# First quarter's modulation weights ahead of the rows; last quarter and gate as two float32r parts; gate in the second group

## The chip, the core and the metric

The kernel runs on one core of one Trainium2 chip. The metric is device time in microseconds, the median of three runs of the whole program: 2112.56 us (2109.44 to 2116.53). A profile of one further execution, with its trace, shows where the time goes. The engines are TensorE (PE, whose weight loads are shown apart as PEld), VectorE (DVE), ScalarE (ACT), GpSimd (POOL) and SyncE (SP), which issues nearly all transfers.

## The reference, cut to what matters

One inference step of one layer over 2048 prompt rows and 8 x 16 sample rows, all float32, width 1024. Nine conditioning vectors `c` (one for the prompt, eight for the samples) give a scale, a shift and a gate for every channel:

```python
mod = silu(c) @ w_ada + b_ada                 # (9, 3072), w_ada is 1024 x 3072
shift, scale, gate = split(mod, 3)
h = rmsnorm(x, norm_g) * (1 + scale) + shift  # needs scale and shift
z = h @ w_in + b_in                           # u, v, gate_a, glu_a, glu_b, gate_b, merge_a, merge_b
v_n = layernorm(gelu(v))
y_a = (gelu(u) * spatial(v_n) * silu(gate_a)) @ w_o_a
y_b = (silu(layernorm(conv31(glu_a * sigmoid(glu_b)))) * silu(gate_b)) @ w_o_b
m = sigmoid(merge_a) * y_a + sigmoid(merge_b) * y_b
y = rmsnorm(x + gate * (m @ w_out), final_g)  # needs gate
```

So `scale` and `shift` are wanted before the first product of the whole kernel, and `gate` only by the last stage of each group of rows.

## The kernel before, in words

**Rows and groups.** Activations lie transposed, channels on the partitions, in eight blocks of 128 channels (k = 0 to 7). The rows go in three groups (`GROUPS`): 768 prompt rows, 768 prompt rows, and 128 sample with the last 512 prompt rows. For each group `prepare` makes h (L772 to L811), `first_products` makes v, the gated convolution and the seven wide products, `branch_a`, `branch_b` and `output` do the rest. These products are numbered in steps from 1 on: the first group's stage of u and ga has the steps 33 to 48, the second group's products with w_in have 81 to 152, and their last stage (ma, mb, gb) 129 to 152.

**Arithmetic.** A product is either one float32 matmul, or several float32r matmuls on values written as the sum of a high and a low part. Nearly all products run on such parts (hh, hl, lh); the parts are made by one ACT and one DVE instruction (`halved`, `split`).

**The modulation.** `ada(name, q, ...)` (L470 to L518) makes one quarter (256 channels, so two blocks k) of scale, shift or gate: three transfers of `w_ada` (3, 3 and 2 blocks of 128 x 256 float32), the product with the nine vectors, an ACT copy out of PSUM, a small transpose by a matmul with `fold`, and two DVE instructions into `mod_scale`, `mod_shift` or `mod_gate`. The product has two forms. With `whole` each block is one float32 matmul of `cin` (9 columns) with 256 columns of weights (L482). Without it ACT writes the high part of the loaded weights (L487), DVE the low part (L489), and each block is two float32r matmuls of `cr`, the high and low parts of the nine vectors side by side (18 columns), with these (L496). In the kernel before all twelve calls are `whole`, so that `cr` is made and not used.

**Order.** All work is recorded as operations with an engine, a cost, what is read and written, a due time and at times a step before which it may not start (`nb`). `Plan.run` (L140) walks the five engines with a model of time and takes at each moment, on each engine, the ready operation of the smallest due time. The order is then fixed: each engine executes its queue strictly in that order, SP included, whose transfers wait in line behind any transfer that has to wait for a buffer. Operations that are due late (the 31 taps of the convolution on DVE, L947 and L951) fill what the model leaves free. Tiles come from a pool of 47 slots (`u`), and 9 units hold weights in parts (`ws`).

**The table that the change touches.** `ADA` gives for each quarter a due time and the forms of scale and shift. `XD = -6` is the due time of the loads of the group's rows (`load_x`, L746), and a quarter's transfers are due when its products are:

```python
ADA = [(-3, True, True), (-1.5, True, True), (-0.5, True, True), (0.5, True, True)]
GATE_AT = 36          # gate's four quarters: due at the steps 36, 40, 44, 48
```

Of the kernel before, what the change touches and what calls it, by code (L numbers as in the profile page):

```python
# [15 lines left out]
P = 128  # L16
D = 1024
# [15 lines left out]

ADA = [(-3, True, True), (-1.5, True, True), (-0.5, True, True), (0.5, True, True)]

# [6 lines left out]
CONV_STEP = (10, 10, 7)  # L42
GATE_AT = 36
LN_DUE = -6
# [213 lines left out]
def encoder_kernel(ctx: ExitStack, tc: tile.TileContext, xT, hist0, cT, w_ada, w_cols, w_v,  # L258
# [14 lines left out]
    op = plan.op  # L273
# [55 lines left out]
    cin = kv([P, KC, 9], "cin")  # L329
    cr = K([P, KC, 18], "cr", F32R).v  # L330
# [8 lines left out]
    def dma(out_fn, in_ap, writes, nbytes, due=0.0, nb=-1, reads=(), extra=0.0):  # L339
        return op("sp", nbytes / 340e3 + extra, lambda: nc.sync.dma_start(out=out_fn(), in_=in_ap),  # L340
                  writes=writes, reads=reads, due=due, nb=nb, lat=3.5)
# [7 lines left out]
    def new_step():  # L349
# [7 lines left out]
       reads=[vec], writes=[vec], due=-9)  # L357
    op("pool", 0.5, lambda: make_identity(nc, ident.t), writes=[ident])
    op("dve", 0.1, lambda: nc.vector.tensor_tensor(fold.t, ident.t[:, :9], ident.t[:, 9:18], op=ALU.add),
       reads=[ident], writes=[fold], due=-9)  # L360
    op("pool", 0.3, lambda: nc.gpsimd.memset(ones.t, 1.0), writes=[ones])
    op("act", 0.3, lambda: nc.scalar.activation(ones_r.t, ones.t, AF.Copy), reads=[ones], writes=[ones_r],
       due=-6)
    op("pool", 0.2, lambda: nc.gpsimd.memset(half.t, -0.5), writes=[half])
    op("act", 0.3, lambda: nc.scalar.activation(cin.t, cin.t, AF.Silu), reads=[cin], writes=[cin],
       due=-9, func="silu")
# [101 lines left out]
    AW = 256  # L468

    def ada(name, q, at, due, whole):  # L470


        ps = bank(f"ada{name}{q}")
        for ks in (range(0, 3), range(3, 6), range(6, 8)):
            m = len(ks) * AW
            w = slot("wa")
            dma(lambda w=w, m=m: w.t[:, :m], w_ada[:, at + ks[0] * AW:at + ks[0] * AW + m], [w], m * P * 4, due=due,
                nb=due - 2 if name == "gate" else -1)
            if whole:
                def mm4(w=w, ks=ks):  # L480
                    for z, k in enumerate(ks):
                        nc.tensor.matmul(ps.t[:9, :AW], cin.t[:, k, :], w.t[:, z * AW:(z + 1) * AW],  # L482
                                         start=(k == 0), stop=(k == KC - 1))
                op("pe", len(ks) * 0.22, mm4, reads=[w, cin], writes=[ps], due=due)
                continue
# [7 lines left out]
            def mm(wh=wh, wl=wl, ks=ks):  # L493
                for z, k in enumerate(ks):
                    for i, x in enumerate((wh, wl)):
                        nc.tensor.matmul(ps.t[:18, :AW], cr.t[:, k, :], x.t[:, z * AW:(z + 1) * AW],  # L496
                                         start=(k == 0 and i == 0), stop=(k == KC - 1 and i == 1))
            op("pe", len(ks) * 0.22, mm, reads=[wh, wl, cr], writes=[ps], due=due)
        a = slot("ada")
# [807 lines left out]
    for q in range(4):  # L1307
        due, scale_whole, shift_whole = ADA[q]
        ada("scale", q, 4 * q * D, due, scale_whole)
        ada("shift", q, (4 * q + 2) * D, due, shift_whole)  # L1310
    h = prepare(0, due=0, nb=-1, dr=DR)
    mixing_setup()
    for q in range(4):
        ada("gate", q, (16 + 2 * q) * D, GATE_AT + 4 * q, True)

# [74 lines left out]
```

## Time and profile before

| | |
|---|---|
| median of 3 runs | 2112.56 us (2109.44 to 2116.53) |
| the profiled execution | 2110.4 us, of which its span, first to last instruction, 2108.7 us |
| mean granted TensorE clock | 0.992 of full speed |
| PE busy | 2060.6 us, 98% |
| DVE busy | 1693.0 us, 80% |
| ACT busy | 931.0 us, 44% |
| memory traffic | 255 GB/s over the span |

The program is bound by TensorE nearly throughout. TensorE's first instruction stands at 14.46 us, so this is most of its idle time. Matmuls are pipelined and the end of one is modelled, so what a matmul costs is read from the start of one to the start of the next, not from its own duration. In the trace each float32 matmul of `ada` has two records, so that "x6" is a chunk of three.

### The profile page before, as it was taken

How to read it: one execution, taken by the hardware profiler on the slowest of the kernel's cores; microseconds unless marked ns; L12 is line 12 of the kernel's file. 1: busy time of each engine (PE TensorE's matmuls, PEld its weight loads, DVE VectorE, ACT ScalarE, POOL GpSimd, SP SyncE). 2: the span in 40 equal slices, each digit the busy share in tenths (PEclk: the TensorE clock that was granted, in tenths of full speed). 3: DMA queues.
4: the chain of work that ended last, by engine and by line, in shares of the span. 5: the costliest groups of instructions: out<-in, count | busy, mean ns of one | idle time of the engine just before them, and what ended most of it. 6: DMA issues, size and time to landing. Idle time of an engine off the chain costs nothing.

```text
span 2108.7 us, 33303 instructions
## 1 busy us (share of the span) xinstructions
PE 2060.6 (98%) x12810; PEld 1966.2 (93%) x12810; DVE 1693.0 (80%) x2407; ACT 931.0 (44%) x1356; POOL 89.5 (4%) x107
## 2 busy tenths in 40 slices
PE   7999999999999999999999999999999999999997
PEld 3999998999979999999998889999999999888997
DVE  5759988999899969688547899769999974956855
ACT  3354455455642343444446432434544544523432
POOL 0000000000100000000001010000000011010000
PEclk9999999999999999999999999999999999999998
DMA  8538777688975477887889876599989999376463
GB/s 328 205 141 295 260 298 270 225 312 294 318 252 204 137 264 247 279 262 246 285 262 324 312 218 181 174 342 335 335 300 319 335 314 342 119 232 221 154 196 118
DMA packets 190927, 540.58 MB, mean 256 GB/s; under 512 B 22064, under 2 KB 39728, under 8 KB 190768
## 3 DMA queue, kind: packets, MB, share of 16 engines
q1 hardware_dynamic: 180256, 511.11, 68.3%
q0 software_dynamic: 10512, 27.33, 7.4%
q8 instruction: 101, 1.65, 0.3%
q14 instruction: 58, 0.48, 0.1%
HBM read 375.47 MB, written 162.89 MB: 255 GB/s over the span
## 4 chain that ended last, share of the span: by engine, by line
PE 87%; DMA 6%; DVE 3%; issue 2%; ACT 0%; SPq 0%; POOL 0%; POOLq 0%; DVEq 0%; ACTq 0%
PE v L1032 9%; PE ob L615 9%; PE out L615 7%; PE bga L660 5%; PE bgla L660 5%; PE bu L660 5%; PE oa L615 4%; PE bglb L660 4%; PE bma L660 4%; PE bmb L660 4%; PE acga L660 3%; PE acu L660 3%; PE acgla L660 3%; PE acma L660 3%; PE bgb L660 3%; PE acglb L660 3%
## 5 line engine op out<-in xcount | busy, mean ns | idle before, releaser
L951 DVE SCALAR_TENSOR_TENSOR dw<-gb,cw,dw 128x768 f32<-128x768 f32 (+1 forms) x720 | 658.5, 924 | 37.8 <-ACT dw L936 32.2
L384 DVE TENSOR_TENSOR w<-ra,w 128x1024 fp32r<-128x1024 f32 x112 | 121.6, 1087 | 37.3 <-ACT w L382 36.3
L382 ACT ACTIVATE wh<-wr 128x1024 fp32r<-128x1024 f32 x88 | 91.9, 1053 | 133.7 <-PE ob L615 76.5
L382 ACT ACTIVATE w<-ra 128x1024 fp32r<-128x1024 f32 x112 | 105.6, 947 | 61.6 <-PE acgla L660 17.4
L384 DVE TENSOR_TENSOR wl<-wr,wh 128x1024 fp32r<-128x1024 f32 x88 | 106.9, 1216 | 3.3 <-ACT wh L382 3.3
L384 DVE TENSOR_TENSOR w<-rb,w 128x512 fp32r<-128x512 f32 x112 | 75.4, 685 | 40.6 <-ACT w L382 40.4
L382 ACT ACTIVATE w<-rb 128x512 fp32r<-128x512 f32 x112 | 67.9, 626 | 77.5 <-PE acglb L660 13.0
L947 DVE SCALAR_TENSOR_TENSOR dw<-gsb,cw,dw 128x128 f32<-128x128 f32 x240 | 82.5, 344 | 0.9 <-ACT dw L940 0.9
L1047 ACT ACTIVATE v<-v 128x768 f32<-128x768 f32 (+1 forms) x24 | 19.4, 810 | 110.4 <-DVE v L1043 94.4
L691 ACT ACT_TABLE_LOAD x50 | 64.2, 1283 | 0.9
L1230 DVE TENSOR_TENSOR mbb<-ob,mbb 128x768 f32<-128x768 f32 (+1 forms) x24 | 21.8, 910 | 51.0 <-PE ob L615 51.0
L671 ACT ACTIVATE u<-bu,vec 128x384 f32<-128x384 f32 (+1 forms) x48 | 26.9, 561 | 58.7 <-PE bu L660 58.6
L671 ACT ACTIVATE glb<-bglb,vec 128x384 f32<-128x384 f32 (+1 forms) x48 | 27.0, 562 | 57.4 <-PE bglb L660 57.0
L671 ACT ACTIVATE gla<-bgla,vec 128x384 f32<-128x384 f32 (+1 forms) x48 | 27.0, 563 | 51.3 <-PE bgla L660 48.0
L671 ACT ACTIVATE ga<-bga,vec 128x384 f32<-128x384 f32 (+1 forms) x48 | 26.9, 560 | 47.4 <-PE bga L660 46.7
L671 ACT ACTIVATE ma<-bma,vec 128x384 f32<-128x384 f32 (+1 forms) x48 | 27.0, 562 | 44.5 <-PE bma L660 43.0
L671 ACT ACTIVATE gb<-bgb,vec 128x384 f32<-128x384 f32 (+1 forms) x48 | 26.9, 561 | 35.9 <-PE bgb L660 33.0
L671 ACT ACTIVATE mb<-bmb,vec 128x384 f32<-128x384 f32 (+1 forms) x48 | 26.8, 559 | 32.6 <-PE bmb L660 32.1
L1277 DVE SCALAR_TENSOR_TENSOR x<-out,mod_gate,x 128x768 f32<-128x768 f32 (+1 forms) x24 | 20.1, 836 | 26.0 <-PE out L615 18.6
L1180 DVE TENSOR_TENSOR mab<-oa,mab 128x768 f32<-128x768 f32 (+1 forms) x24 | 21.7, 906 | 20.6 <-DMA mab<-away_ma__232 5.6
L382 ACT ACTIVATE w<-rs 128x1024 fp32r<-128x1024 f32 x28 | 29.6, 1056 | 16.0 <-DVE rs L445 9.2
L384 DVE TENSOR_TENSOR w<-rs,w 128x1024 fp32r<-128x1024 f32 x28 | 34.1, 1220 | 3.1 <-ACT w L382 1.1
(1068 smaller groups left out, 7190.5 us busy)
## 6 DMA issues: line engine op xcount, KB each, us to landing
w<-kept SPq DMA_DIRECT2D x224, 512.0 KB, 5.4
kept<-w SPq DMA_DIRECT2D x112, 512.0 KB, 4.0
ra<-in_w_cols SPq DMA_DIRECT2D x84, 512.0 KB, 6.6
wr<-in_w_cols SPq DMA_DIRECT2D x80, 512.0 KB, 6.2
rb<-in_w_cols SPq DMA_DIRECT2D x28, 512.0 KB, 5.9
rb<-in_w_cols SPq DMA_DIRECT2D x56, 256.0 KB, 5.3
x<-in_xT SPq DMA_DIRECT2D x32, 384.0 KB, 7.4
wa<-in_w_ada SPq DMA_DIRECT2D x24, 384.0 KB, 7.0
```

Source lines behind the costliest of these rows:

```text
L382: op("act", c_act(n, 0.1), lambda: nc.scalar.activation(hi_ap(), src_ap(), AF.Copy), reads=[src], writes=[hi], due=due)
L384: op("dve", c_dve(n), lambda: nc.vector.tensor_tensor(lo_ap(), src_ap(), hi_ap().bitcast(F32), op=ALU.subtract), reads=[src, hi], writes=[ ...
L615: nc.tensor.matmul(ps.t[:, z, :cw_], a.t[:, ks], b.t[:, c0:c0 + cw_], start=first and i == 0, stop=last and i == 2)
L660: nc.tensor.matmul(acc(), a.t[:, o + k * P:o + (k + 1) * P], b.t[:, xo:xo + nh], start=first and k == 0 and i == 0, stop=k == 3 and i == 2 ...
L671: op("act", c_act(nh, 0.28), lambda: nc.scalar.activation(half(i, z), B(), f, bias=col(bias, i)), reads=[bk, vec], writes=[out[i].part(z)] ...
L691: op("act", c_act(nh), lambda: nc.scalar.activation(half(1, 1), half(1, 1), func), reads=[out[1].part(1)], writes=[out[1].part(1)], due=st ...
L947: op("dve", c_dve(ns), lambda q=q: nc.vector.scalar_tensor_tensor(dw.t[:, :ns].rearrange("p (s l) -> p s l", l=LS), g3()[:, :, q:q + LS], ...
L951: op("dve", c_dve(npr), lambda q=q: nc.vector.scalar_tensor_tensor(dw.t[:, ns:n], g.t[:, q:q + npr], cw.t[:, j, q:q + 1], dw.t[:, ns:n], o ...
L1032: nc.tensor.matmul(o(), a.t[:, sl], view(b)[:, k % 4, :], start=state["n"] == 0, stop=state["n"] == 3 * KC - 1, skip_group_check=True)
L1180: op("dve", c_dve(n), lambda m=m, b=(lambda ps=ps, m=m: banks(ps, m, n)): nc.vector.tensor_tensor(b()[1], b()[0], b()[1], op=ALU.mult), re ...
L1230: op("dve", c_dve(n), lambda m=m, b=(lambda ps=ps, m=m: banks(ps, m, n)): nc.vector.tensor_tensor(b()[1], b()[0], b()[1], op=ALU.mult), re ...
L1277: op("dve", c_dve(bn), lambda j=j, x=x, ps=ps, bn=bn: nc.vector.scalar_tensor_tensor(x.t[:, :bn], ps.t.rearrange("p a b -> p (a b)")[:, :b ...
```

## The change

Four edits, with no other line touched:

1. `ADA_LOAD` gives the transfers of a quarter a due time of their own. For the first quarter it is -8 and -7.9, ahead of the rows' -6; for the other three it is what it was.
2. The last quarter of scale and shift is no longer `whole`.
3. All four quarters of gate are no longer `whole`, and are due at the steps 131, 135, 139 and 143, in place of 36 to 48.
4. The model's cost of a block becomes 0.43 (whole) and 0.24 (parts), in place of 0.22 for both.

```diff
-ADA = [(-3, True, True), (-1.5, True, True), (-0.5, True, True), (0.5, True, True)]
+ADA = [(-3, True, True), (-1.5, True, True), (-0.5, True, True), (0.5, False, False)]
+
+ADA_LOAD = [(-8, -7.9), (-1.5, -1.5), (-0.5, -0.5), (0.5, 0.5)]
...
-GATE_AT = 36
+GATE_AT = 131
...
-    def ada(name, q, at, due, whole):
+    def ada(name, q, at, due, whole, load=None):
...
-            dma(lambda w=w, m=m: w.t[:, :m], w_ada[:, at + ks[0] * AW:at + ks[0] * AW + m], [w], m * P * 4, due=due,
-                nb=due - 2 if name == "gate" else -1)
+            dma(lambda w=w, m=m: w.t[:, :m], w_ada[:, at + ks[0] * AW:at + ks[0] * AW + m], [w], m * P * 4,
+                due=due if load is None else load, nb=due - 2 if name == "gate" else -1)
...
-                op("pe", len(ks) * 0.22, mm4, reads=[w, cin], writes=[ps], due=due)
+                op("pe", len(ks) * 0.43, mm4, reads=[w, cin], writes=[ps], due=due)
...
-            op("pe", len(ks) * 0.22, mm, reads=[wh, wl, cr], writes=[ps], due=due)
+            op("pe", len(ks) * 0.24, mm, reads=[wh, wl, cr], writes=[ps], due=due)
...
-        ada("scale", q, 4 * q * D, due, scale_whole)
-        ada("shift", q, (4 * q + 2) * D, due, shift_whole)
+        ada("scale", q, 4 * q * D, due, scale_whole, ADA_LOAD[q][0])
+        ada("shift", q, (4 * q + 2) * D, due, shift_whole, ADA_LOAD[q][1])
...
-        ada("gate", q, (16 + 2 * q) * D, GATE_AT + 4 * q, True)
+        ada("gate", q, (16 + 2 * q) * D, GATE_AT + 4 * q, False)
```

What the planner makes of it, at three places. Line numbers are two higher in the changed kernel.

SP's queue at the start of the program: before, the eight loads of rows `x` come first, and the first quarter's weights `wa` behind them.

```order
L340 DMA vec<-in_vecs 128x144
L746 DMA x_41_342<-in_xT 128x768
...
L746 DMA x_48_371<-in_xT 128x768
L340 DMA wa_376<-in_w_ada 128x768
L340 DMA wa_381<-in_w_ada 128x768
L340 DMA wa_386<-in_w_ada 128x512
```

And now, the same queue:

```order
L342 DMA vec<-in_vecs 128x144
L342 DMA wa_342<-in_w_ada 128x768
L342 DMA wa_348<-in_w_ada 128x768
L342 DMA wa_350<-in_w_ada 128x512
L342 DMA wa_352<-in_w_ada 128x768
L342 DMA wa_356<-in_w_ada 128x768
L342 DMA wa_363<-in_w_ada 128x512
L748 DMA x_53_366<-in_xT 128x768
```

The six transfers of the first quarter went past the eight of the rows; the order behind these is the same.

TensorE's queue around the first product of the kernel (`v_0_0`, of the first column block of v). Before: `adascale_21` is the third quarter's scale, `adashift_26` its shift, `adascale_31` and `adashift_36` the last quarter's; these stand between or behind the first products of v.

```order
L482 MATMUL adascale_21_526<-wa_508,cin 9x256 x2
L1032 MATMUL v_0_0_134_550<-wh_518,h0h_499 128x256
L1032 MATMUL v_0_0_134_550<-wh_518,h0l_514 128x256
...
L482 MATMUL adashift_26_561<-wa_516,cin 9x256 x3
...
L482 MATMUL adascale_31_608<-wa_554,cin 9x256 x3
...
L482 MATMUL adashift_36_646<-wa_615,cin 9x256 x2
```

Now, with `adascale_31` and `adashift_42` for the last quarter:

```order
L484 MATMUL adascale_21_524<-wa_488,cin 9x256 x2
L484 MATMUL adashift_26_532<-wa_511,cin 9x256 x2
L508 MATMUL adascale_21_524<-fold,ada_572 128x9 x2
L1034 MATMUL v_0_0_170_581<-wh_486,h0h_539 128x256
...
L498 MATMUL adascale_31_613<-wah_564,cr 18x256
L498 MATMUL adascale_31_613<-wal_585,cr 18x256
...
L498 MATMUL adashift_42_709<-wah_631,cr 18x256
L498 MATMUL adashift_42_709<-wal_716,cr 18x256
```

The third quarter's shift moved wholly ahead of the first product of v, and the last quarter is in short matmuls among the products of v.

SP's queue in the second group, as its stage of ma, mb and gb begins; before, kept parts of weights `w` and raw weights `ra` and `rb` follow each other here:

```order
L340 DMA rb_8987<-in_w_cols 128x512
L435 DMA w_9005<-kept_154 128x1024
L435 DMA w_9026<-kept_154 128x1024
L340 DMA ra_9030<-in_w_cols 128x1024
L435 DMA w_9080<-kept_157 128x1024
L340 DMA rb_9083<-in_w_cols 128x512
L435 DMA w_9099<-kept_157 128x1024
L435 DMA w_9131<-kept_157 128x1024
```

And now, from the same `rb` on:

```order
L342 DMA rb_8943<-in_w_cols 128x512
L437 DMA w_8961<-kept_154 128x1024
L437 DMA w_8982<-kept_154 128x1024
L342 DMA ra_8986<-in_w_cols 128x1024
L342 DMA wa_9036<-in_w_ada 128x768
L437 DMA w_9039<-kept_157 128x1024
L437 DMA w_9055<-kept_157 128x1024
L342 DMA wa_9072<-in_w_ada 128x768
L342 DMA wa_9078<-in_w_ada 128x512
```

The twelve transfers of gate, which stood in the first group's stage of u and ga, now stand here among the kept weights.

## Rows read from the trace of the kernel before

**Rows 1.** The page's table of engines: busy us, share of the span, instructions

```profile
PE 2060.6 (98%) x12810; PEld 1966.2 (93%) x12810; DVE 1693.0 (80%) x2407; ACT 931.0 (44%) x1356; POOL 89.5 (4%) x107
```

**Rows 2.** Chain that ended last in 0 to 110: start us, us, what

```profile
5.83 8.50 DMA wa<-in_w_ada
...
14.46 2.72 PE adascale L482 x6
17.18 1.79 PE xs L529 x12
...
28.54 0.37 PE psx L551
...
39.41 0.90 PE v L1032 x6
40.31 1.39 PE adashift L482 x6
...
43.64 0.55 PE v L1032 x3
44.19 0.96 PE adashift L482 x4
...
59.52 0.54 PE adashift L506 x4
60.06 9.83 PE v L1032 x81
```

**Rows 3.** A stretch of 5 us: busy by engine, TensorE's granted clock, DMA share, GB/s

```profile
30.00:35.00 5.00, 4.75 (x23) 2.17 (x22) 3.76 (x6) 1.98 (x4) 0.00 (x0) 1.00 1.04 414
```

**Rows 4.** Timeline of ACT: start us, us, engine line op, operands [idle before]

```profile
11.49 2.75 ACT L773 ACTIVATE xsq<-x 128x768 f32<-128x768 f32 x3 [0.15 <-DMA x<-in_xT]
30.62 0.49 ACT L554 ACTIVATE bcx<-psx 128x384 f32<-128x384 f32 x1 [0.17 <-PE psx L552]
```

**Rows 5.** Timeline of DVE at the start of the program

```profile
10.41 5.21 DVE L776 TENSOR_TENSOR xsum<-xsum,xsq 128x768 f32<-128x768 f32 x5 [1.22 <-ACT xsq L773]
...
23.17 0.48 DVE L513 TENSOR_SCALAR mod_scale<-adascale,vec 128x9 f32<-128x9 f32 x2 [2.29 <-PE adascale L506]
...
61.58 1.01 DVE L810 SCALAR_TENSOR_TENSOR h6l<-x,mod_shift,h6h 128x768 fp32r<-128x768 f32 x1
62.51 1.01 DVE L810 SCALAR_TENSOR_TENSOR h7l<-x,mod_shift,h7h 128x768 fp32r<-128x768 f32 x1
...
72.84 0.42 DVE L1039 TENSOR_TENSOR v<-v,bvA 128x256 f32<-128x256 f32 x1 [0.66 <-PE v L1032]
```

**Rows 6.** Timeline of PE: one chunk of gate among float32r products; the stall at 70 us

```profile
70.39 0.39 PE L1032 MATMUL v<-wh,h2h 128*128 128x256 f32 x1 [0.52 <-DVE v L1039]
...
277.29 0.34 PE L660 MATMUL acga<-h3h,w 128*128 128x384 f32 x1
277.55 1.46 PE L482 MATMUL adagate<-wa,cin 128*9 128x256 f32 x6
278.95 0.44 PE L660 MATMUL bga<-t3h,w 128*128 128x384 f32 x1
279.23 0.34 PE L660 MATMUL bga<-t3l,w 128*128 128x384 f32 x1
```

**Rows 7.** Longer stretches: group one's gates, its neighbours, group two's last stage

```profile
277.40:393.00 115.60, 115.60 (x625) 101.45 (x624) 99.53 (x131) 58.71 (x85) 1.05 (x1) 1.00 0.74 267
...
450.00:500.00 50.00, 50.00 (x287) 50.00 (x286) 47.95 (x60) 28.39 (x41) 0.84 (x1) 1.00 0.70 253
...
1000.00:1050.00 50.00, 50.00 (x288) 50.00 (x287) 27.19 (x30) 21.18 (x30) 0.86 (x1) 1.00 0.87 284
```

**Rows 8.** Transfers on the page: KB each, median us from issue to landing

```profile
wa<-in_w_ada SPq DMA_DIRECT2D x24, 384.0 KB, 7.0
```

**Rows 9.** Stretches of 10 us around the step from group one to two

```profile
580.00:590.00 10.00, 6.94 (x27) 5.36 (x26) 5.38 (x6) 4.75 (x7) 0.00 (x0) 0.73 1.05 329
590.00:600.00 10.00, 10.00 (x55) 8.73 (x55) 10.00 (x12) 6.83 (x8) 0.00 (x0) 0.93 1.03 413
```

## The prediction

> **What bounds the kernel now.** I read the page's table of engines first: PE is busy for 98% of the span and DVE for 80% [rows 1], so a change pays where it takes time from TensorE's queue, or from a wait in front of it. Next comes the chain that ended last in the first 110 us [rows 2]. Until 14.33 us it is a wait for the first `wa`, and from 14.46 us nearly all PE: float32 chunks of the modulation, first alone, then, from the first product of v at 39.34 us on, between products of v. Two matters are to be seen in it. A float32 chunk of three blocks takes 1.39 us and one of two 0.96, while a float32r matmul with the same 256 columns takes 0.12 us (81 in 9.83). And v is held up by queue order: modulation stands ahead of it and in it. Third, the stretch of the four gates, 277 to 393 us [rows 7]: PE is busy for all 115.6 us, so what leaves it there is time. The first of the chunks in it [rows 6] shows what one really costs.
>
> Times below are made against the profiled execution: 2110.4 us, of which 2108.7 are its span. The median shown, 2112.56 us, is 2.2 us more; I subtract the gain from the median.
>
> **Gate: removed from the first group.** A product of 384 columns takes 0.17 us from start to start (0.34 for two). The product before the chunk starts at 277.29, so the next one would start at 277.46; it starts at 278.95, and its successor 0.28 later, 0.11 more than usual [rows 6]. The chunk thus costs 278.95 - 277.46 + 0.11 = 1.60 us, which is 1.39 and 0.21 for the change of form. By the same 0.2, a chunk of two costs 1.16 and the pair of small transposing matmuls 0.75 (0.54 and 0.2). A quarter is 1.60 + 1.60 + 1.16 + 0.75 = 5.1 us, and four are 20.4 us of PE out of the first group.
>
> Added to the second group: per quarter 16 float32r matmuls of 256 columns, 16 x 0.12 = 1.92 us, with no change of form, and the same 0.75 for the transpose: 2.7 us, four times 10.7. Net on PE: **9.8 us saved**. The trace has no float32r matmul with 18 columns of weights. Its bounds are 0.12 us, the row of the same 256 columns with 128 columns of weights, and the float32 block's 1.39 / 3 = 0.46. I take 0.12: only the width of the weights differs.
>
> What hides the rest: in the second group each quarter adds three ACT and three DVE instructions (0.9, 0.9 and 0.6 us, by the 0.93 of a DVE instruction of 768 elements [rows 5] and the 0.92 of ACT's squares [rows 4]), some 10 us each over four quarters. DVE is busy for 27.2 of 50 us there and ACT for 21.2 [rows 7], PE for all 50. If that cover were gone, it would cost up to these 10 us. In the first group DVE, 99.5 of 115.6 us now, gets a stage some 20 us shorter, so about 96% busy. That is what 450 to 500 us shows already, 47.95 of 50 with PE at 50.00 [rows 7], so I take all 20.4 us. The order also sends six convolution taps out of that stage to later ones.
>
> **First quarter's weights ahead of the rows.** The six transfers are 2.1 MB, 5.2 us at the 0.4 MB per us that the start shows [rows 3]. The rows' loads come that much later: the last sum of squares, now done at 15.62 [rows 5], is done near 20.8. The second quarter's first weights are the fifteenth large transfer in place of the ninth, so 14.33 + 5.2 = 19.6 us. What PE gets for it is the first quarter's 7.5 us (twice 1.39 + 1.39 + 0.96) between 5 and 18 us, where it mostly stood still.
>
> From 19.6 us PE's queue runs without a pause, by the new order: second quarter 7.5; sums of the squares 1.8; four broadcasts 1.1 (0.37 + 0.18, twice); two transposes 1.1; third quarter, now scale and shift, 7.5; one transpose 0.5. That is 19.5 us, with the changes of form 19.9: the first product of v is at **39.5 us**, 0.2 later than before. Its operands are there: the broadcast ends near 31.5 (before at 31.1 [rows 4]), because the later rows meet a wait that is gone, 2.29 us in which DVE stood at `mod_scale` ahead of the broadcast's operands [rows 5].
>
> **Last quarter in parts.** What counts is how much modulation is left behind the first product. Before: nine chunks (six of 1.39, three of 0.96), four transposes of 0.54 and ten returns to v at 0.2 each (0.55 for three matmuls instead of 0.35) [rows 2]: 8.3 + 2.9 + 2.2 + 2.0 = 15.4 us. As a check, v's first column block ends at 72.7 [rows 5]: 33.4 us are 144 x 0.12 = 17.3 of v, 15.4, and a stall of 0.6 [rows 6]. After: three transposes with their returns, 2.2, and 32 parts at 0.12, 3.8: 6.0 us. The gain is 15.4 - 6.0 - 0.2 = **9.2 us**.
>
> Its cover is DVE. From 31.5 us on it has sixteen instructions for h and six low parts (14.9 + 5.0 at 0.93 and 0.62), two low parts of weights (2.4) and the modulation's small ones (1.5): done at 55.3, with its waits for the transposes by 57. PE first wants the last h behind 108 products of the lower six blocks and the 6.0 us, at 39.5 + 13.0 + 6.0 = 58.5. Before, the last h was done at 63.5. So 1.5 us are to spare; past that, each us that DVE is late costs one, at most the 5.0 of the new low parts. The DVE work that was done before 63 and is now behind it (some 3 us of sums for the combined operands) meets the later column blocks of v, where DVE waits for PE.
>
> **Two rules to weigh.** While all engines only load, the trace moves 414 GB/s [rows 3]. The Trainium skill (DMA: Bandwidth & Descriptors, Specifications) gives a core some 358 GB/s from memory; by this the 2.1 MB would take 5.9 us and the sum would lose 0.7. The trace disagrees, and I stay with the row. The other rule is about the clock, and a rival below.
>
> **Sum.** 9.8 + 9.2 = 19.0 us: span 2089.7, execution 2091.4, and on the median 2112.56 - 19.0 = **2093.6 us**.
>
> **Rivals.**
> - *TensorE's clock falls in the new gaps.* Now PE works early, then has a gap of some 2 us before 19.6. In the trace, in a stretch where PE stood for 3.1 of 10 us, the granted clock was 0.73 of full speed and in the next ten 0.93 [rows 9]: a mix of the 1.2 and 2.4 GHz levels that cost 2.7 + 0.7 = 3.4 us. The first chunk of the kernel took 2.72 in place of 1.39 [rows 2], though the granted clock reads full there. So 1.3 to 3.4 us are lost at 19.6: up to 2097.0. Against it: the gap is short. The Trainium skill (TensorE: Matmul & The Clock Gate, HAM oscillation — how this bites in real kernels) has a rule for it, that idle gaps of TensorE throttle its clock to half until it has been busy for a while; rows 9 agree.
> - *The rows come too late.* If the row statistics hold PE's queue at the sums or the broadcast, the 5.2 us of delay reach the first product: 2098.8. For it: all of h hangs on them. Against it: PE has modulation to do until 29 us.
> - *Gate's transfers collide.* Here SP's queue waits for PE to free weight units, memory moves 284 GB/s at 0.87 share [rows 7], and one `wa` takes 7.0 us to land [rows 8]. An ACT instruction that waits for it holds up the copies out of PSUM behind it, a transfer ahead of kept weights delays these. 4.2 MB at 0.39 are 10.8 us if none of it is hidden: 2104.4. Against it: the order places parts several products ahead of their use, and the same transfers in the first group cost PE nothing [rows 7].
> - *DVE becomes the bound.* If DVE's 16.1 idle us in the first group's stage [rows 7] are latencies that stay, little of the 20.4 comes out (1.6, the eight small instructions), while the second group still pays 10.7, and the start keeps 63.5 - 57 = 6.5: 2.6 us slower, 2115.2. It decides once DVE's work there exceeds the 95 us that PE has left. Against it: the neighbours at 96%.
> - *An 18-column part costs what a float32 block does* (slower). At 0.46, a quarter costs 16 x 0.34 = 5.4 us more than taken, six of them 32.6: 13.6 us slower, 2126.2. The point of no gain is 0.12 + 19.0 / 96 = 0.32 us a matmul. Against it: float32r with 128 columns of weights runs at 0.12.
>
> **How the numbers follow.** Forecast 0.64 (its own range 2089 to 2098), clock 0.08, rows 0.08, transfers 0.08, DVE 0.07, dear parts 0.03, rest 0.02. The range 2087 to 2105 takes in the first four and, downward, a first product a few us earlier together with a median as near to the profiled run as 2.2 us allow. A measurement of this kernel tells 0.3%, 6.3 us, from no change: faster is below 2106.2. That is the first four and little else, 0.87; DVE and what lies near it are the same, 0.09; slower 0.04.
>
> **What would show it.** In the profile after: PE's first chunk near 5 us; the first product of v at 39 to 40; DVE's last copy of v's first block near 63.5 in place of 72.8; no modulation on PE between 260 and 380; parts 0.12 apart in the second group, and PE still busy for 50 of 50 us there. Wrong would be a first product past 42, PE waits for `wal` or for h6 and h7, a clock under 1.00 between 15 and 40, or PE idle where gate's parts stand.

## The result

Four runs of the changed kernel took 2097.66 us in the median (2094.37 to 2099.14), four of the kernel before 2113.61: the ratio is 0.9924, with 0.9908 to 0.9941 as its 95% interval. That is 16.0 us, 12.5 to 19.4, less. 2093.6 was predicted. The profiled run took 2096.98 us, its span 2095.1 against 2108.7: 13.6 us, and the traces account for these.

Where they came from is read from the starts of the same instructions in both timelines of PE. All times are us from the start of the span. "v" is the first product of v, "bglb" the first of the seven wide products of a group, "bu" the first product of the first group's u, "oa" the first product of the first group's output of branch a, "sums" the column sums of the second group's rows (`xs`).

| first start of | v | bglb, group 1 | bu | oa | sums | bglb, group 2 | bglb, group 3 | end of span |
|---|---|---|---|---|---|---|---|---|
| before | 39.34 | 123.99 | 254.22 | 566.45 | 602.84 | 716.80 | 1343.74 | 2108.7 |
| after | 44.48 | 119.00 | 249.01 | 541.47 | 580.40 | 694.60 | 1331.67 | 2095.1 |
| lead | -5.1 | 5.0 | 5.2 | 25.0 | 22.4 | 22.2 | 12.1 | 13.6 |

So the start gave 5.0, the first group without its gates 20.0 (5.0 to 25.0); the step to the second group took 2.8, the gates in the second group 10.1; the last 1.5 come behind the third group's bglb, a stretch that takes from 762.1 to 766.2 us in the profiles of this study whatever the edit: this spread is no smaller, so they are not put down to the change.

**The profile after.** The page's table of engines, as in [rows 1], shows PE with 10.7 us less work and DVE with 14.1 more:

```profile
PE 2049.9 (98%) x12810; PEld 1970.5 (94%) x12810; DVE 1707.1 (81%) x2425; ACT 940.6 (45%) x1374; POOL 97.3 (5%) x107
```

The chain that ended last in the first 60 us answers to [rows 2] (start, us, what):

```profile
3.13 5.95 DMA wa<-in_w_ada
9.13 2.73 PE adashift L484 x6
...
18.13 0.65 issue
18.78 0.35 DVE mod_shift L520 x2
19.13 0.88 DVE xsum L778
...
22.23 0.97 DVE xsum L778
23.33 2.69 PE xs L531 x12
26.02 2.66 PE adascale L484 x6
28.68 2.10 PE adashift L484 x6
...
37.00 1.39 PE adascale L484 x6
...
44.55 0.90 PE v L1034 x6
...
54.10 0.69 PE adashift L498 x6
```

Two things are new in it. From 18 to 23 us the chain runs over DVE, which adds up the squares of the rows, and no longer over PE. And behind it PE is slow: the sums take 2.69 us (1.79 before), a chunk 2.66 (1.39 at 37.00). Stretches of the same trace (us, busy PE, PEld, DVE, ACT, POOL, TensorE's granted clock, DMA share, GB/s) show why, and answer to [rows 9]:

```profile
15.00:20.00 5.00, 3.62 (x20) 1.94 (x19) 2.99 (x7) 3.96 (x7) 0.00 (x0) 1.00 1.03 414
20.00:25.00 5.00, 3.25 (x12) 1.98 (x11) 2.87 (x3) 0.34 (x1) 0.00 (x0) 0.50 1.07 388
25.00:30.00 5.00, 5.00 (x15) 2.29 (x16) 2.24 (x5) 0.00 (x0) 1.34 (x1) 0.50 1.04 409
30.00:35.00 5.00, 4.73 (x23) 2.10 (x21) 1.96 (x4) 2.64 (x4) 0.00 (x0) 0.98 1.04 414
272.20:371.30 99.10, 99.10 (x568) 99.10 (x567) 95.18 (x120) 57.80 (x82) 1.05 (x1) 1.00 0.76 274
1000.00:1050.00 50.00, 50.00 (x293) 48.81 (x292) 31.99 (x39) 23.81 (x35) 0.00 (x0) 1.00 0.79 261
570.00:580.00 10.00, 3.27 (x20) 2.62 (x18) 10.00 (x12) 5.53 (x8) 0.00 (x0) 0.82 1.02 390
580.00:590.00 10.00, 9.60 (x43) 8.68 (x44) 9.88 (x14) 0.78 (x1) 2.06 (x1) 0.67 0.70 249
```

The granted clock is at its lower level, 1.2 of 2.4 GHz, from 20.0 to 30.2 us. Ahead of this PE had stood still for 1.3 us (until 19.39); the clock fell 0.6 us into the chunk that followed, so that the second stop, 1.75 us ahead of the sums, came when it was low already. It rose with PE at work without a stop since 23.33. The stretch 272.2 to 371.3 is the old place of the gates [rows 7]: PE is busy for all of it, DVE for 96%. From 1000 to 1050 the gates stand in it, and PE is busy for 50 of 50. From 570 on lies the step between the groups, with PE idle for 6.7 of 10 us.

The gate's parts on PE's timeline, in place of the chunk in [rows 6], start 0.12 us apart, and the product behind them starts 0.12 after the last; its own successor, at 963.90, keeps the usual 0.18:

```profile
962.85 0.34 PE L662 MATMUL bmb<-t23h,w 128*128 128x384 f32 x1
963.02 0.28 PE L498 MATMUL adagate<-wah,cr 128*18 128x256 f32 x1
963.13 0.28 PE L498 MATMUL adagate<-wal,cr 128*18 128x256 f32 x1
...
963.60 0.28 PE L498 MATMUL adagate<-wal,cr 128*18 128x256 f32 x1
963.72 0.34 PE L662 MATMUL acmb<-h0h,w 128*128 128x384 f32 x1
```

### The profile page after: what moved, and what is told of

Read it like the earlier page. It is cut to its first block, busy times and chain, and to the rows that moved or that the text cites. A ratio compares the mean times of both kernels' runs of the same rounds, so it can differ in the third digit from the quotient of the medians.

```text
span 2095.1 us, 33328 instructions
## 1 busy us (share of the span) xinstructions
PE 2049.9 (98%) x12810; PEld 1970.5 (94%) x12810; DVE 1707.1 (81%) x2425; ACT 940.6 (45%) x1374; POOL 97.3 (5%) x107
## 4 chain that ended last, share of the span: by engine, by line
PE 87%; DMA 7%; DVE 4%; issue 1%; ACT 0%; SPq 0%; DVEq 0%; POOLq 0%; ACTq 0%
PE v L1034 9%; PE ob L617 9%; PE out L617 7%; PE oa L617 5%; PE bu L662 5%; PE bga L662 5%; PE bglb L662 4%; PE bma L662 4%; PE bgla L662 4%; PE bgb L662 4%; PE bmb L662 4%; PE acu L662 3%; PE acga L662 3%; PE acglb L662 3%; PE acma L662 3%; PE acgla L662 3%
## 5 line engine op out<-in xcount | busy, mean ns | idle before, releaser
L953 DVE SCALAR_TENSOR_TENSOR dw<-gb,cw,dw 128x768 f32<-128x768 f32 (+1 forms) x720 | 657.0, 922 | 21.3 <-ACT dw L938 16.2
L1049 ACT ACTIVATE v<-v 128x768 f32<-128x768 f32 (+1 forms) x24 | 19.4, 810 | 103.1 <-DVE v L1045 89.6
L384 ACT ACTIVATE w<-rs 128x1024 fp32r<-128x1024 f32 x28 | 29.6, 1057 | 18.5 <-DVE rs L447 10.9
```

What stands on the lines that cost most here:

```text
L384: op("act", c_act(n, 0.1), lambda: nc.scalar.activation(hi_ap(), src_ap(), AF.Copy), reads=[src], writes=[hi], due=due)
L953: op("dve", c_dve(npr), lambda q=q: nc.vector.scalar_tensor_tensor(dw.t[:, ns:n], g.t[:, q:q + npr], cw.t[:, j, q:q + 1], dw.t[:, ns:n], o ...
```

## The experiments

Two questions were open: which edit gave what, and what took 4.2 us at the start and 2.8 between the groups. The table has the first starts of the same instructions, us, and the times; a ratio is to runs of the kernel before on the same chip.

| kernel | v | bglb 1 | oa | sums | bglb 2 | bglb 3 | span | median | ratio, interval |
|---|---|---|---|---|---|---|---|---|---|
| last_only | 38.84 | 118.02 | 560.33 | 597.16 | 710.10 | 1336.09 | 2101.2 | 2103.17 | 0.9958, 0.9945 to 0.9970 |
| gate_only | 41.09 | 125.72 | 548.90 | 587.55 | 702.89 | 1339.22 | 2102.5 | 2104.22 | 0.9966, 0.9954 to 0.9979 |
| rows_first | 33.88 | 117.66 | 540.01 | 579.59 | 694.13 | 1331.16 | 2093.3 | 2097.89 | 0.9937, 0.9923 to 0.9950 |
| gate_whole | 40.03 | 114.56 | 537.02 | 575.92 | 690.12 | 1336.94 | 2102.4 | 2106.97 | 0.9975, 0.9963 to 0.9986 |
| gate_early | 44.81 | 119.34 | 554.75 | 593.21 | 708.12 | 1336.31 | 2099.9 | 2100.11 | 0.9938, 0.9925 to 0.9952 |
| warm | 43.76 | 118.29 | 540.78 | 579.27 | 694.23 | 1332.10 | 2097.6 | 2097.93 | 0.9936, 0.9923 to 0.9949 |
| warm_all | 43.04 | 117.57 | 540.13 | 579.63 | 694.86 | 1332.19 | 2095.8 | 2097.81 | 0.9925, 0.9912 to 0.9938 |
| after_again | 44.03 | 118.56 | 541.03 | 580.03 | 694.15 | 1330.74 | 2095.6 | 2099.00 | 0.9935, 0.9922 to 0.9948 |
| prep7 | 45.14 | 119.67 | 542.14 | 583.98 | 692.69 | 1329.30 | 2093.6 | 2094.32 | 0.9918, 0.9903 to 0.9934 |
| rows_first_prep7 | 34.23 | 118.00 | 540.32 | 582.02 | 692.03 | 1327.27 | 2090.3 | 2092.77 | 0.9910, 0.9896 to 0.9924 |
| rows_first_prep8 | 34.45 | 118.22 | 540.55 | 587.69 | 693.57 | 1328.81 | 2095.0 | 2097.00 | 0.9928, 0.9915 to 0.9942 |
| three_parts | 37.72 | 118.85 | 541.90 | 583.47 | 693.83 | 1330.90 | 2095.9 | 2094.73 | 0.9913, 0.9898 to 0.9928 |

The profiled run and the median of a kernel differ by up to 2 us and more, so differences of a few us are read from the timelines, where each stands at its place, and the ratios say whether a measurement tells them.

### The edits one by one

**last_only** is the kernel before with the second edit.

```
-ADA = [..., (0.5, True, True)]
+ADA = [..., (0.5, False, False)]
```

> The kernel before with the second edit alone: only the fourth quarter of the scale and shift in two float32r parts. Theory A (the start's gain is the product work that the parts save): 7.1 us of float32 chunks become 3.8 us of parts, the first product of bglb in the first group comes 3.3 us earlier than in the kernel before, some of it is lost again between the groups, 2109 to 2111 us. Rival B (the planner's new cost figures, edit four, bring part of the start's 6.3 us that the kernel without the first edit shows): the same 3.3 us here, and the rest is theirs. Rival D (the parts save more than their count says, since the halves of the rows come sooner): bglb 5 to 6.5 us earlier, 2105 to 2108.

bglb comes 6.0 us earlier, and the ratio makes it 8.9 us (6.3 to 11.6): more than theory A's, and nearest to D, whose 2105 to 2108 the time of 2103.17 still misses. Between the first product of v and bglb the starts of PE add up to 11.24 us of chunks before and 3.75 of chunks with 3.72 of parts here: 3.8 less. The 576 products of v take 70.74 and 69.56: 1.2 less, since the first matmul of v behind a float32 chunk takes 0.22 us to the next one instead of 0.12 (43.57 to 43.79 in the kernel before). The stall of 0.52 in [rows 6] is gone, and v begins 0.5 earlier. That is the 6.0. The last 0.5 is no effect of the edit: PE's first chunk began 0.3 sooner in this run, at 14.16, and the column sums took 0.2 less at the same order. So the parts are worth 5.5 here.

**gate_only** is the kernel before with the third edit.

```
-GATE_AT = 36
+GATE_AT = 131
...
-        ada("gate", q, (16 + 2 * q) * D, GATE_AT + 4 * q, True)
+        ada("gate", q, (16 + 2 * q) * D, GATE_AT + 4 * q, False)
```

> The kernel before with the third edit alone: the gate in two float32r parts and in the second group. Theory A: 20.0 us go out of the first group, 11.3 come into the second, and some 2.8 are lost between the groups, where TensorE comes to the second group's column sums before the rows' squares are summed: 2107.7 us. Rival B (the loss between the groups belongs to the first two edits' 5 us): 2104.9. Rival D (the gate alone makes up nearly all of the gain): under 2101.

0.9966: 7.2 us (4.4 to 9.7), nearest to B. But the loss between the groups is there: from bglb to oa 19.3 us are gained (442.46 to 423.18), between oa and the second bglb 3.6 are lost (150.35 to 153.99), and the second group pays 9.4 (626.94 to 636.33). The 2.8 us of the changed kernel thus do not come from the first two edits; B had the time nearly right for a wrong reason. Nor does the gate's new place explain them: in gate_early below, with the gate's parts at their old place, the same stretch still loses 3.0 (554.75 to 708.12). What the runs with the loss share is a first group that is 7 us or more shorter from bglb to oa. In last_only, where it is as long as before (442.31), nothing is lost. In the profile of gate_only bglb came 1.7 us later than in the kernel before, at the same order: the first group's column sums, at 16.56, took 2.72 us and not 1.79, since PE stayed at half speed longer, though the granted clock reads 1.00 there.

**rows_first** is the changed kernel without the first edit.

```
-ADA_LOAD = [(-8, -7.9), ...]
+ADA_LOAD = [(-3, -3), ...]
```

> The changed kernel without its first edit: the first quarter's weights are again loaded behind the rows, the rest stays. Theory A (the first edit is worth little here, since its gaps let the clock fall and the rows come later): the first product of v at 39 to 40 us, some 12 us of modulation behind it, 1.7 us slower than the changed kernel, near 2099.4. Rival B (the first edit is worth the 5.9 us that the prediction's 9.2 leave beside the last quarter's 3.3): near 2103.5. Rival D (the first edit costs more than it gives): under 2096.

bglb at 117.66 is 1.3 us earlier than in the changed kernel, and the time is the same within the intervals. Theory A's cause holds, its size does not: the first edit gives nothing. v came at 33.88, not at 39 to 40, since here more chunks stand behind it than theory A counted on: it is 83.78 us from v to bglb, 74.52 in the changed kernel. Together with last_only, whose bglb is at 118.02, this says that the start's gain is the last quarter's parts, and that the planner's cost figures (edit four) give the start nothing that can be told (0.4 us).

**gate_whole** is the changed kernel with the gate in float32 chunks at its new place (`GATE_AT + 4 * q, True`).

> The changed kernel with the gate left in whole float32 chunks, at its new place in the second group: place without parts. Theory A (the second group pays for every chunk, as the first did): the gate costs 20.0 to 20.4 us there instead of 11.3, the time rises by 8.7 to 9.1, to 2106.5 us. Rival B (the second group has cover for the gate, and its 11.3 us have another cause): within 2 us of the changed kernel. Rival D (the parts' copies and subtractions on ScalarE and VectorE cost part of what the products save): a rise of 5 to 8.

From the second group's bglb to the third's it is 646.82 us, 637.07 in the changed kernel, 626.94 in the kernel before: the whole gate costs 19.9 there, the parts 10.1. Theory A holds: the second group has no cover, parts save 9.8, place alone saves nothing (20.0 out, 19.9 in). This run's start was a find: the same start program as in the changed kernel, but bglb at 114.56. More on it below.

**gate_early** is the changed kernel with the parts at the gate's old place (`GATE_AT = 36`).

> The changed kernel with the gate's two float32r parts back at their old place in the first group: parts without the move. Theory A (TensorE pays for the products wherever they stand, the parts alone saved the 8.7 to 9.3 us, and the move itself gave nothing, as the whole gate cost 19.9 in the second group and 20.0 in the first): 10.2 to 11.3 us of gate in the first group, none in the second, and no 7 us of waiting at the second group's column sums, where TensorE would now come 10 us later: 2093 to 2098 us. Rival B (VectorE, busy 99.5 of 115.6 us in that part of the first group, cannot take the parts' subtractions too): TensorE waits there, the first group ends 4 us or more later than theory A says, 2101 to 2106.

2.1 us above theory A's range. From bu (249.35) to oa it is 305.40 us, against 292.46 with no gate there: 12.9 for the parts, where A had 10.2 to 11.3. The 64 parts take 7.47, their transposes 2.15, two stalls of PE 1.4, for ScalarE's copies of u; the other 1.9 is spread over the products around. VectorE was busy for 48.0 and 47.8 of two stretches of 50 us and held nothing up: rival B's mechanism isn't seen. The wait at the second group's sums, which A wanted gone, is still 5.4 us. Against the changed kernel beside it (0.9935) the ratio 0.9938 tells no difference, and the medians are 1.1 us apart. The traces show more: from bglb of the first group to that of the third it is 1216.97 us here, against 1212.67 and 1212.18 in the two profiles of the changed kernel. What the move adds to the parts is thus open, between nothing and some 5 us.

### What took the start's gain

Five profiles (the changed kernel, after_again, prep7, gate_early, gate_whole) have the same order of work on PE at the start. Two things stand out in them.

*The queue of ACT and DVE.* ACT's timeline of the changed kernel (start, us, engine line op, operands, idle before and what ended it):

```profile
12.60 1.79 ACT L775 ACTIVATE xsq<-x 128x768 f32<-128x768 f32 x2
16.04 0.37 ACT L503 ACTIVATE ada<-adascale 9x256 f32<-9x256 f32 x1 [1.65 <-PE adascale L484]
16.32 0.82 ACT L775 ACTIVATE xsq<-x 128x768 f32<-128x768 f32 x1
17.05 0.36 ACT L503 ACTIVATE ada<-adashift 9x256 f32<-9x256 f32 x1
17.32 3.03 ACT L775 ACTIVATE xsq<-x 128x768 f32<-128x768 f32 x4
```

and DVE's:

```profile
13.48 2.03 DVE L778 TENSOR_TENSOR xsum<-xsum,xsq 128x768 f32<-128x768 f32 x2 [9.00 <-ACT xsq L775]
17.51 0.48 DVE L515 TENSOR_SCALAR mod_scale<-adascale,vec 128x9 f32<-128x9 f32 x2 [2.01 <-ACT ada L503]
17.91 0.95 DVE L778 TENSOR_TENSOR xsum<-xsum,xsq 128x768 f32<-128x768 f32 x1
18.78 0.35 DVE L520 TENSOR_SCALAR mod_shift<-adashift,vec 128x9 f32<-128x9 f32 x2
19.05 4.14 DVE L778 TENSOR_TENSOR xsum<-xsum,xsq 128x768 f32<-128x768 f32 x4
```

The first three squares start as their rows land; the other five do not wait for rows any more. The first quarter's copy out of PSUM stands ahead of five squares, and `mod_scale` ahead of five sums; both wait for PE, which works on the first quarter at half speed until some 13 us (2.73 for a chunk, though the granted clock reads 1.00). The last sum ends near 23.2. In gate_whole, where PE was done with the first quarter 1.9 us sooner, all eight squares start as their rows land, and the last sum ends at 21.3:

```profile
15.60 3.62 ACT L775 ACTIVATE xsq<-x 128x768 f32<-128x768 f32 x4
17.13 4.13 DVE L778 TENSOR_TENSOR xsum<-xsum,xsq 128x768 f32<-128x768 f32 x4
```

So the queue costs 1.9 us. No run changes the order on ACT and DVE alone; this rests on the two profiles. Without the first edit the squares run to 13.9 as their rows land, and the sums to 15.3.

*The clock behind it.* From the start of the sums to the first product of v it is 21.15 us in the changed kernel, 21.06 in after_again, and 17.97 in gate_whole, with the same instructions. PE's timeline in gate_whole:

```profile
9.17 1.46 PE L484 MATMUL adashift<-wa,cin 128*9 128x256 f32 x6 [1.15 <-DMA wa<-in_w_ada]
...
19.41 2.72 PE L484 MATMUL adascale<-wa,cin 128*9 128x256 f32 x6 [3.06 <-DMA wa<-in_w_ada]
22.06 1.60 PE L531 MATMUL xs<-ones,xsum 128*128 128x1 f32 x12
...
40.03 0.39 PE L1034 MATMUL v<-wh,h0h 128*128 128x256 f32 x1
```

and its stretches:

```profile
18.00:20.00 2.00, 0.59 (x2) 0.27 (x3) 1.79 (x3) 1.11 (x2) 0.00 (x0) 0.72 1.03 410
20.00:25.00 5.00, 5.00 (x24) 2.58 (x23) 1.32 (x3) 0.00 (x0) 0.99 (x1) 0.77 1.07 386
25.00:30.00 5.00, 5.00 (x25) 2.07 (x22) 3.48 (x7) 2.27 (x3) 0.35 (x1) 1.00 1.04 409
```

Here the clock came up at the second chunk (1.46), so the first quarter was done 1.9 us sooner, and was low only from 18.9 to 22.3 us, behind a stop of PE and in it: one chunk paid (2.72). v at 40.03 and a start 9.4 us shorter (123.99 to 114.56) are what was predicted, 39.5 and 9.2.

**warm** puts idle products into the two gaps ahead of the sums, with PSUM columns of the second quarter's scale, whose values so lack a chunk:

```
+                    if name == "scale" and q == 1 and ks[0] == 0:
+                        for _ in range(20):
+                            nc.tensor.matmul(ps.t[:, AW:]..., ones_r.t, ones_r.t..., start=True, stop=True, ...)
...
+            if name == "shift" and q == 0:
+                for _ in range(10):
+                    nc.tensor.matmul(ps.t[:, :AW]..., ones_r.t, ones_r.t..., start=True, stop=True, ...)
```

> The changed kernel with idle work for TensorE added: ten float32r products of 256 columns on the matrix of ones behind the first quarter's last transposes, twenty behind the first chunk of the second quarter's scale, all into columns of PSUM that nobody reads. They stand in the two gaps (1.3 and 1.8 us) ahead of the column sums of the first group's rows; every other instruction keeps its place. Theory C (the start lost its gain to the clock): no stretch between 15 and 40 us falls below 1.00, the column sums still begin near 23.3, take 1.8 instead of 2.69 us, the two chunks behind them 1.4 and 1.3 instead of 2.66 and 2.10, and the first product of v comes near 41.6 instead of 44.5: 3 us less, 2094.7 us. Rival R (the rows are late and DVE's adds and halves set the start): the clock holds but the first product of v stays at 44 to 44.6 and the time within 1 us of the changed kernel. If the added products outlast the gaps, the column sums begin later than 23.5.

The sums began at 24.30, past the 23.5 that was set as the sign of added products outlasting the gaps. The chunks behind the sums take 1.46 as expected, but the clock fell at 34.1 us instead, where PE waits twice ahead of the broadcast (0.3 and 0.5 us): the next chunk took 2.71, and v came at 43.76. Neither theory: the fall was moved, not removed.

**warm_all** fills these gaps too, in columns that nobody reads or that are overwritten (ten products, twenty-five ahead of the sums in their bank, five).

> The changed kernel with idle products for TensorE in all the gaps of the start: ten behind the first quarter's last transposes, twenty-five ahead of the column sums in their own bank (which they then overwrite), five behind the second quarter's transposes. Theory C: the clock stays at 1.00 from 15 to 40 us, the column sums take 1.5 to 1.8 us, the chunks 1.3 to 1.4, and the first product of v comes at 40 to 42 us; the time 2 to 4 us below the changed kernel run beside it. Rival R (the rows are late): v not before 43.5. Rival E (the clock finds another moment to fall, as it did at 34 us with fewer idle products): a slice below 0.9 behind 25 us, and v near 43.5 for that reason.

The clock is 1.00 in every stretch from 15 to 40 us, such as

```profile
20.00:25.00 5.00, 4.90 (x34) 3.66 (x34) 4.11 (x6) 1.11 (x2) 0.00 (x0) 1.00 1.07 386
25.00:30.00 5.00, 5.00 (x30) 2.87 (x31) 2.03 (x5) 0.04 (x1) 1.34 (x1) 1.00 1.04 408
```

and from the start of the sums to v it is 18.14 us, 3.0 less than the 21.15 of the changed kernel: that much is the clock, as theory C has it. But v comes at 43.04, 1.0 past its bound, because the sums began at 24.90:

```profile
18.77 1.46 PE L511 MATMUL adashift<-ones_r 128*128 128x256 f32 x10
20.16 1.46 PE L484 MATMUL adascale<-wa,cin 128*9 128x256 f32 x6
21.55 3.25 PE L535 MATMUL xs<-ones_r 128*128 128x256 f32 x25
24.90 1.47 PE L539 MATMUL xs<-ones,xsum 128*128 128x1 f32 x12
```

The squares' sums were late here as well (the last four, 4.14 us, begin at 20.61), in part by the added products themselves, behind which `mod_shift` waited 0.7 us on DVE, in part by a first quarter that was slower on PE (its copy stands at 16.81 in place of 16.04). Rival R has its share: with the clock held the squares' sums still set where the column sums begin. The time, 0.9925, is not told from the changed kernel's.

**after_again** repeats the changed kernel.

> The changed kernel once more, unaltered, for a second profile of its start and a time beside the other three. Theory C (the start's loss is the clock, and how long it stays low differs from run to run: the same start reached v at 44.5, 45.1 and, with the clock low only from 18 to 22 us, at 40.0): the first product of v somewhere from 40 to 45, and where it is near 40 no slice after 23 us shows less than 1.00. Rival R (the rows set it): v at 44 to 45 whatever the clock shows. The time within 3 us of 2097.7.

v at 44.03, the sums at 22.97, the clock 0.50 from 20 to 25 and 0.53 to 30: theory C's case again, though rival R would have v there too; it is gate_whole and warm_all that part the two. Of five profiles of this start, four have v at 44.0 to 45.1 and one at 40.0.

### What was lost between the groups

PE has one long wait in the changed kernel, where the kernel before lost 2.4 and 0.7 us on transfers and ran [rows 9] at 0.73:

```profile
580.40 2.72 PE L531 MATMUL xs<-ones,xsum 128*128 128x1 f32 x12 [7.13 <-DVE xsum L778]
```

**prep7** moves the second group's preparation one step later in the plan.

```
-    h = prepare(1, due=step_no[0] + PREP_DUE, nb=step_no[0] + PREP_NB)
+    h = prepare(1, due=step_no[0] + 7, nb=step_no[0] + PREP_NB)
```

> The changed kernel with the second group's rows prepared one step later in the plan (the due time of its column sums and of what follows them 7 instead of 6 steps out): on TensorE the sums stand 42 rows of the first branch's products later, some 7.4 us of work. Theory T (the 7.1 us that TensorE waits for the sum of squares at 573 to 580 us are an accident of the order): the wait goes and 3 to 7 us come back by the first product of the second group's bglb; 2091 to 2094.7 us. Rival U (VectorE and the row transfers bound this stretch, so the wait only moves behind the column sums): within 1 us of the changed kernel.

The wait falls from 7.1 to 3.3 us, and from oa to the second bglb it is 150.55 us, against 153.13 in the changed kernel and 150.35 before: 2.6 come back, a little less than theory T's least. The order was the cause of that part; 3.3 us of wait stay. The time, 2094.32, is in theory T's range, but its interval overlaps the changed kernel's.

**rows_first_prep7** is that without the first edit.

> The changed kernel without its first edit and with the second group's rows prepared a step later: the two edits that each shortened a stretch of the trace, together. Theory T (without the first edit the start is 1.3 us shorter, and the 8.3 us that the second group's column sums waited there shrink to 4 or so with the later place): bglb of the second group near 691.4, 2093 us, 4 to 5 under the changed kernel. Rival U (the start's 1.3 us vanish in the wait, which ends when the rows' squares are summed): as the later place alone, 2094.3.

bglb of the second group at 692.03, 2092.77 us, ratio 0.9910 (0.9896 to 0.9924): theory T's time, the lowest of the study. Its interval and the changed kernel's (0.9908 to 0.9941; 0.9922 to 0.9948) overlap; the two were not run side by side, so that it is faster is likely and not shown.

**rows_first_prep8** moves the preparation by one more step (`+ 8`).

> The changed kernel without its first edit and with the second group's rows prepared two steps later instead of one: the column sums stand 90 rows of the first branch later. Theory T (what TensorE still waited there with one step, 1.7 us at the sums and 2.4 at the product behind them, goes too): 2089 to 2092 us. Rival U (the rows' halves now come too late for the second group's v): TensorE waits at v instead, 2093 to 2096.

2097.00 us is above both ranges, by 1.0 above rival U's; the mechanism is rival U's, with the wait at the broadcast rather than at v (engine, line, what it waited for: us in total, times, longest):

```profile
PE psx L553 <- DVE dgx L582: 6.4, 1, 6.4
PE v L1034 <- DVE h7l L812: 0.4, 1, 0.4
```

The wait has moved behind the sums. From oa to the second bglb it is 154.12 us without a later step (rows_first), 151.71 with one and 153.02 with two: one step is the best of the three in the traces, while the times' intervals overlap.

**three_parts** is rows_first_prep7 with the third quarter in parts as well.

```
-ADA = [..., (-0.5, True, True), (0.5, False, False)]
+ADA = [..., (-0.5, False, False), (0.5, False, False)]
```

> The same as the kernel without the first edit and with the later preparation, and the third quarter of scale and shift in two float32r parts as well. Theory A (TensorE bounds the start): another 3.3 us of products saved, bglb of the first group near 114.4, 2090 us. Rival B (VectorE bounds it: it is busy 4.4 to 4.8 of each 5 us from 30 to 40, and six subtractions of 0.6 to 0.9 us come there): TensorE waits for the parts' low halves or for h4 to h7, bglb no earlier than 117, 2093 to 2096.

bglb at 118.85, 0.9 later than without, and 2094.73 us: the numbers of rival B. But this run's start was slow for another reason: the column sums took 2.72 us and the chunks behind them

```profile
19.84 2.73 PE L484 MATMUL adascale<-wa,cin 128*9 128x256 f32 x6
22.36 2.77 PE L484 MATMUL adashift<-wa,cin 128*9 128x256 f32 x6
...
28.96 0.45 PE L553 MATMUL psx<-dgx,ones_r 128*128 128x384 f32 x1
```

where rows_first_prep7 has 1.70, then 1.46 for a chunk, and the first broadcast at 24.93. So PE came to the broadcast 4.0 us later, with the third quarter's form playing no part yet. From the broadcast to bglb it is 89.89 us, against 93.06: 3.2 less, which is theory A's saving, and this with 0.8 us of PE waiting for h6 in it, which is rival B's sign. VectorE has no room there,

```profile
35.00:40.00 5.00, 5.00 (x30) 3.13 (x29) 4.99 (x9) 4.89 (x9) 0.00 (x0) 1.00 1.07 396
40.00:45.00 5.00, 5.00 (x44) 4.68 (x44) 5.00 (x8) 4.12 (x7) 0.00 (x0) 1.00 1.03 403
```

but PE is busy for all of it as well. The four times show no gain; whether the parts would give one behind a start at full speed stays open.

## Why the prediction was right, and where it was not

**The time** was 4.1 us above the forecast, within its range, on the side expected. That it is no further off is in part luck: the medians show 16.0 us of gain, the two profiled spans 13.6, and the traces up to the third group's bglb 12.1, where 19.0 were forecast. The terms that failed miss 4.2 us at the start and 2.8 between the groups.

**Gate out of the first group**: 20.4 predicted, 20.0 measured. **Gate into the second**: 10.7 and 10.1, with parts 0.12 apart and PE at 50 of 50 us, as the step said. The 9.8 net was 9.9. DVE was 96% busy in the shortened stage, as its neighbours had shown, so the rival of DVE as the bound and that of dear parts both fell, and so did the one of colliding transfers: the second group's PE shows no new wait on them.

**The start**: 9.2 predicted, 5.0 measured. What is left behind the first product was right: from v to bglb it is 74.52 us in the changed kernel, which is 69.1 of v, 3.8 of parts and the transposes, and DVE's last copy of v's first block began at 68.53, 24 us after v, as predicted (39.5 to 63.5). h7 was done at 62.0, and PE waited for none of h or the low parts. The step that failed is "From 19.6 us PE's queue runs without a pause", at both ends of it. It took the last sum of squares to be done near 20.8, from the transfers alone, so that the column sums would follow the second quarter's first chunk at 21.0: they began at 23.33, 2.3 us later. 1.9 of these are the modulation's copies, which stand ahead of squares and sums on ACT and DVE and wait for a PE at half speed; in gate_whole, without that delay, the last sum ended at 21.3, close to the forecast. And from the column sums to v it counted the other 18.5 us: they were 21.15, because the clock was at its lower level until 30.2 us, 2.65 more. The two make up the 5.0 by which v was later than 39.5. The rival of rows that come too late had the first of them, with the wrong cause: from the fourth on no square waited for its row.

The clock was the first rival, priced at 1.3 to 3.4 us with a chance of 0.08. Its price held, 3.0 by warm_all, and its chance was too small: the clock fell in all five profiles of this start, for 10.2 us in four and for 3.4 in gate_whole. The reason given against it, that the gap is short, was wrong: in the changed kernel the stop ahead of the fall was 1.3 us long. The rule of the Trainium skill that the prediction set beside it (TensorE: Matmul & The Clock Gate, HAM oscillation — how this bites in real kernels), that idle gaps throttle the clock until TensorE has been busy for a while, agrees with the 0.50 here, and with warm_all, in which the gaps are filled and no stretch from 15 to 40 us is below 1.00.

The sum for the first two edits was made as one, 15.4 to 6.0 us; the runs part it. The last quarter's parts alone give 5.5 to 6.0 us at bglb, the first quarter's early loads 3.1 us in the one profile where the clock was low only briefly, and -0.9 to -2.0 in the others (bglb at 114.56, and at 118.56 to 119.67, against 117.66 without them). The early work on PE is bought with gaps and half speed.

**The step between the groups** was not in the sum, and took 2.8. Which instruction of the second group PE meets first was not asked: PE comes 25.0 us earlier, but the rows' first square only 24.3 (587.87 to 563.57), the second 23.3, and the last of their sums 22.4 (601.83 to 579.40), with one convolution tap more among the sums on a DVE that is busy for 10 of 10 us. PE's gain above that becomes a wait. gate_early, whose first group is shorter with the gate still in it, has the same four taps there and loses 3.0; last_only has three, as the kernel before, and loses nothing.

## What to carry to other kernels

Work moved to the front of a queue has to be priced at the clock and behind the instructions that it then meets: ask for each engine what now stands ahead of the chain that sets the start, and what waits in it. A move that takes time out of one stage is worth it only as far as the next stage's inputs come earlier too; read when they land, not only when PE is free. And where one edit both makes work cheaper and moves it, run the two apart: here the whole chunks cost 20.0 us at the old place and 19.9 at the new one, so the move alone gave nothing, while the cheaper form took 9.8 off at the new place.

## What the runs showed of the hardware

- TensorE's speed at the start differs from run to run at the same order of work: the second chunk of the kernel took 1.46 us in one profile and 2.73 in four, though the granted clock reads 1.00 there in all, and behind that the granted clock was 0.50 to 0.58 from 20 to 30 us in four, 0.77 from 20 to 25 us and 1.00 behind that in one. Without the early loads the column sums took 1.5 to 1.8 us in most profiles and 2.72 in two (gate_only, three_parts). A difference of a few us in one profile's start has to be read with this beside it.
- Filling some of the gaps moved the fall (a chunk of 2.71 us at 35 us) instead of removing it; with all of them filled it stayed away, in one profile each.
- A float32r product of 18 columns of weights with 256 columns takes the 0.118 us that one of 128 columns does, and changes nothing for its neighbours, where a float32 chunk also cost the products of v behind it: 0.123 us each among nine chunks, 0.120 without any.
